# A row normalization on one core: a three-row first tile ahead of the 12-row tiles

## The chip, the cores and the metric

The kernel runs on one core of a Trainium2 chip. Times are microseconds of device time of one execution; the profile and its trace come from one profiled execution.

## What is computed

Every row of 1024 numbers is divided by the sum of its absolute values. There are 32 x 512 = 16,384 rows of float32, 67.1 MB in and 67.1 MB out.

```
x = randn(32, 512, 1024)                      # float32
sums = sum(abs(x), axis=-1, keepdims=True)
out = x / (sums + 1e-8)
```

## The kernel before

The 16,384 rows are spread over 128 partitions, so each partition has 128 rows to do. A tile takes R = 12 rows of each partition (128 x 12 x 4 KB, 6.3 MB): ten tiles of 12 rows and a last one of eight (`rows`). `piece(flat, i)` cuts tile i out of the flat tensor in such a way that the k rows of a partition lie side by side in memory, so that each partition's part of a transfer is one run of k x 4 KB.

The pool `sbuf` has four buffers of 12 rows (4 x 48 KB per partition), the pool `stats` small ones for the row sums. For each tile, in the order of the loop at the end of the function:

- SP issues the load into the next buffer (L72). Loads are alone on SP's queue. The fifth and later ones wait until the store of the tile four places earlier has landed, since that frees their buffer.
- VectorE reduces the tile to row sums of absolute values (L45), adds the small constant (L52), takes the reciprocal (L54), and multiplies the first half of the rows in place by it (L55; six of twelve rows).
- ScalarE multiplies the other rows in place, one instruction for each row (L62), and then issues the store of the tile (L74). Loads and stores so are on two queues, q1 from SP and q10 from ScalarE.

The order on each engine is the program's own (`tc.manual_schedule()`); nothing is reordered. DMA semaphores are taken from a set of eight and used again. The profile's numbers for a transfer count packets: each partition's run is one, 48 KB for a 12-row tile, and each of the 16 DMA engines carries eight of them for each transfer and ends it with a packet of four bytes for the semaphore.

Of the kernel before, what the change touches and what calls it, by code (L numbers as in the profile page):

```python
# [1 line left out]

# [4 lines left out]

FP32 = mybir.dt.float32
EPS = 1e-8


@with_exitstack
def kernel(
    ctx: ExitStack,
    tc: tile.TileContext,
    x: bass.AP,
    out: bass.AP,
):
    nc = tc.nc
    P = nc.NUM_PARTITIONS  # L20

    x_flat = x.flatten_outer_dims()
    out_flat = out.flatten_outer_dims()
    n, d = x_flat.shape


    R = 12
    BUFS = 4
    per_partition = n // P
    assert n % P == 0  # L30
    rows = [R] * (per_partition // R)
    if per_partition % R:
        rows.append(per_partition % R)

    def piece(flat, i):
        a, k = P * sum(rows[:i]), rows[i]
        return flat[a : a + P * k, :].rearrange("(p r) d -> p r d", p=P)

    sbuf = ctx.enter_context(tc.tile_pool(name="sbuf", bufs=BUFS))
    stats = ctx.enter_context(tc.tile_pool(name="stats", bufs=4))  # L40

    def normalize(x_tile, r0, k, kv):

        s = stats.tile([P, R], FP32)
        nc.vector.tensor_reduce(  # L45
            out=s[:, :k],
            in_=x_tile[:, r0 : r0 + k, :],
            axis=mybir.AxisListType.X,
            op=mybir.AluOpType.add,
            apply_absolute_value=True,  # L50
        )
        nc.vector.tensor_scalar_add(out=s[:, :k], in0=s[:, :k], scalar1=EPS)  # L52
        inv = stats.tile([P, R], FP32)
        nc.vector.reciprocal(out=inv[:, :k], in_=s[:, :k])  # L54
        nc.vector.tensor_mul(  # L55
            out=x_tile[:, r0 : r0 + kv, :],
            in0=x_tile[:, r0 : r0 + kv, :],
            in1=inv[:, :kv].unsqueeze(2).to_broadcast([P, kv, d]),
        )
        for r in range(kv, k):  # L60
            row = x_tile[:, r0 + r, :]
            nc.scalar.activation(  # L62
                out=row,
                in_=row,
                func=mybir.ActivationFunctionType.Copy,
                scale=inv[:, r : r + 1],
            )

    with tc.manual_schedule():
        for i, k in enumerate(rows):  # L70
            x_tile = sbuf.tile([P, R, d], FP32)
            nc.sync.dma_start(out=x_tile[:, :k, :], in_=piece(x_flat, i))  # L72
            normalize(x_tile, 0, k, k // 2)
            nc.scalar.dma_start(out=piece(out_flat, i), in_=x_tile[:, :k, :])  # L74


# [1 line left out]
_INS = ['x']  # L78
_OUTS = [((32, 512, 1024), 'float32')]


# [23 lines left out]
```

## Time and profile before

| what | before |
|---|---|
| median of 4 runs | 317.63 us (317.23 to 317.84) |
| the profiled execution | 317.3 us, its span 315.7 us |
| VectorE busy | 212.4 us, 67% of the span |
| ScalarE busy | 69.0 us, 22% |
| read from and written to HBM | 67.11 MB each, 425 GB/s over the span |
| the first load, issue to landing | 17.9 us |
| first store issued at | 38.78 us after the span's start |
| last store issued at | 295.13 us |
| load of 12 rows (6144 KB), issue to landing, median | 38.6 us |
| store of the same size, issue to landing, median | 53.3 us |

The span is the part of an execution between the first and the last instruction that the profiler saw; the execution's own time is 1.6 us longer. A landing time contains the waiting behind earlier transfers of the same queue, so it is much longer than the transfer. In the view of stretches, "GB/s" is what the DMA engines moved in that stretch, reading and writing together: a byte that is loaded or stored counts once, and the DMA share is the mean busy share of the 16 DMA engines. Packets are counted whole, so a stretch of a few microseconds can show a share a little above one.

### The profile page before, as it was taken

To read this page: it belongs to the slowest core of one execution; us is meant where nothing else is said; L and a number is where in the kernel's file an instruction comes from. 1 tells how busy PE (TensorE), PEld (TensorE's weight loads), DVE (VectorE), ACT (ScalarE), POOL (GpSimd) and SP (SyncE) were. 2 spreads that over 40 slices of the span, in tenths; PEclk is the share of its full clock that TensorE was granted. 3 is DMA by queue.
4 is the path that set the end of the run, shared out by engine and by line. 5 is a ranking of instruction groups with operands and counts; after the bars stand their busy time and mean duration, and the time that the engine had idled before them with its cause. 6 is when DMAs were issued, how large, how long until landed. Compare 5 with 4: busy or idle time off the path is not lost.

```text
span 315.7 us, 227 instructions
## 1 busy us (share of the span) xinstructions
DVE 212.4 (67%) x44; ACT 69.0 (22%) x65; POOL 0.2 (0%) x4
## 2 busy tenths in 40 slices
DVE  0069999999499079719944991797099449949300
ACT  0010804308007000700340070007003400611300
POOL 0000000000000000000000000000000000000000
DMA  8999999999999999999999999999999999999996
GB/s 305 480 405 430 461 380 424 405 473 417 405 480 411 411 473 411 424 455 424 436 436 424 437 448 411 430 442 424 436 448 411 436 428 448 436 440 436 417 430 282
DMA packets 3169, 134.23 MB, mean 425 GB/s; under 512 B 352, under 2 KB 352, under 8 KB 352
## 3 DMA queue, kind: packets, MB, share of 16 engines
q1 hardware_dynamic: 1584, 67.11, 49.8%
q10 hardware_dynamic: 1584, 67.11, 49.1%
q14 instruction: 1, 0.01, 0.0%
HBM read 67.11 MB, written 67.11 MB: 425 GB/s over the span
## 4 chain that ended last, share of the span: by engine, by line
DMA 55%; DVE 25%; another core or an unknown queue 9%; ACT 4%; issue 0%; SPq 0%; DVEq 0%; ACTq 0%
DMA x_tile<-in_x_dram 41%; DVE s L45 19%; DMA out_dram<-x_tile 14%; DVE x_tile L55 6%; ACT x_tile L62 4%; DVE inv L54 0%; DVE s L52 0%; SPq L72 0%; DVEq L54 0%; ACTq L74 0%
## 5 line engine op out<-in xcount | busy, mean ns | idle before, releaser
L45 DVE TENSOR_REDUCE s<-x_tile 128x12 f32<-128x12288 f32 (+1 forms) x11 | 138.2, 12564 | 81.0 <-DMA x_tile<-in_x_dram 81.0
L62 ACT ACTIVATE x_tile<-x_tile,inv 128x1024 f32<-128x1024 f32 x64 | 67.7, 1135 | 207.2 <-DVE inv L54 207.2
L55 DVE TENSOR_TENSOR x_tile<-x_tile,inv 128x6144 f32<-128x6144 f32 (+1 forms) x11 | 70.0, 6364 | 0.4
L62 ACT ACT_TABLE_LOAD x1 | 1.3, 1283 | 18.7 <-DMA x_tile<-in_x_dram 18.7
L54 DVE RECIPROCAL inv<-s 128x12 f32<-128x12 f32 (+1 forms) x11 | 2.5, 226 | 0.9
L52 DVE TENSOR_SCALAR s<-s 128x12 f32<-128x12 f32 (+1 forms) x11 | 1.9, 173 | 0.4
L89 POOL MEMSET const-bfloat16-1.0<- 128x1 bf16 x1 | 0.1, 101 | 0.0
L89 POOL MEMSET const-uint8-127<- 128x1 uint8 x1 | 0.1, 101 | 0.0
L89 POOL MEMSET const-float32-0.0<- 128x1 f32 x1 | 0.1, 98 | 0.2 <-issue 0.2
L89 POOL MEMSET const-float32-1.0<- 128x1 f32 x1 | 0.1, 98 | 0.0
## 6 DMA issues: line engine op xcount, KB each, us to landing
x_tile<-in_x_dram SPq DMA_DIRECT2D x10, 6144.0 KB, 38.6
out_dram<-x_tile ACTq DMA_DIRECT2D x10, 6144.0 KB, 53.3
x_tile<-in_x_dram SPq DMA_DIRECT2D x1, 4096.0 KB, 33.3
out_dram<-x_tile ACTq DMA_DIRECT2D x1, 4096.0 KB, 19.5
```

What stands on the lines that cost most here:

```text
L45: nc.vector.tensor_reduce(out=s[:, :k], in_=x_tile[:, r0 : r0 + k, :], axis=mybir.AxisListType.X, op=mybir.AluOpType.add, apply_absolute_v ...
L52: nc.vector.tensor_scalar_add(out=s[:, :k], in0=s[:, :k], scalar1=EPS)
L54: nc.vector.reciprocal(out=inv[:, :k], in_=s[:, :k])
L55: nc.vector.tensor_mul(out=x_tile[:, r0 : r0 + kv, :], in0=x_tile[:, r0 : r0 + kv, :], in1=inv[:, :kv].unsqueeze(2).to_broadcast([P, kv, d]),)
L62: nc.scalar.activation(out=row, in_=row, func=mybir.ActivationFunctionType.Copy, scale=inv[:, r : r + 1],)
L89: nc = _bacc.Bacc("TRN2", target_bir_lowering=False, num_devices=1)
```

## The change

The row list begins with a tile of three rows; the rest, 125 rows, is cut into ten tiles of 12 and a last one of five. The three-row tile has a buffer of its own in a new pool, so that the four 12-row buffers are free for the next four tiles. There are twelve tiles instead of eleven. Half of the rows, rounded down, go to VectorE as before: one of three in the first tile, two of five in the last.

```diff
     R = 12
     BUFS = 4
-    per_partition = n // P
+
+    FIRST = 3
     assert n % P == 0
-    rows = [R] * (per_partition // R)
-    if per_partition % R:
-        rows.append(per_partition % R)
+    full, last = divmod(n // P - FIRST, R)
+    rows = [FIRST] + [R] * full + ([last] if last else [])
...
     sbuf = ctx.enter_context(tc.tile_pool(name="sbuf", bufs=BUFS))
+    first = ctx.enter_context(tc.tile_pool(name="first", bufs=1))
     stats = ctx.enter_context(tc.tile_pool(name="stats", bufs=4))
...
         for i, k in enumerate(rows):
-            x_tile = sbuf.tile([P, R, d], FP32)
+            if i == 0:
+                x_tile = first.tile([P, FIRST, d], FP32)
+            else:
+                x_tile = sbuf.tile([P, R, d], FP32)
             nc.sync.dma_start(out=x_tile[:, :k, :], in_=piece(x_flat, i))
             normalize(x_tile, 0, k, k // 2)
             nc.scalar.dma_start(out=piece(out_flat, i), in_=x_tile[:, :k, :])
```

## The prediction

> **What bounds the kernel now.** I read the page's head and parts 2 and 3 first, since they say which resource is never free.
>
> ```profile
> span 315.7 us, 227 instructions
> DVE 212.4 (67%) x44; ACT 69.0 (22%) x65; POOL 0.2 (0%) x4
> ...
> DMA  8999999999999999999999999999999999999996
> ...
> q1 hardware_dynamic: 1584, 67.11, 49.8%
> q10 hardware_dynamic: 1584, 67.11, 49.1%
> ```
>
> VectorE is idle a third of the span and ScalarE three quarters, while the DMA row is full from the first slice to the last but one. The loads (q1) and the stores (q10) fill 49.8% + 49.1% = 98.9% of the time of 16 DMA engines: 312.2 of 315.7 us. The other 3.5 us are mostly the head before the first byte and the end after the last. Both queues moved the same bytes in the same packets, but the loads took 0.7% of 315.7 = 2.2 us longer per engine: this is the only waste inside the stream.
>
> Next come the stretches, to see whether a phase with loads alone is slower than one with both directions. The last two columns are the DMA share and GB/s.
>
> ```profile
> core 0: us, DVE busy (x) ACT busy (x) POOL busy (x), PEclk, DMA share, GB/s
> 0.00:1.70 1.70, 0.00 (x0) 0.00 (x0) 0.20 (x4) 1.00 0.00 0
> 1.70:16.20 14.50, 0.00 (x0) 0.00 (x0) 0.00 (x0) 1.00 1.05 431
> 16.20:40.00 23.80, 21.22 (x5) 7.62 (x7) 0.00 (x0) 1.00 0.99 430
> 40.00:45.00 5.00, 5.00 (x1) 0.00 (x0) 0.00 (x0) 1.00 0.96 324
> ...
> 112.20:141.20 29.00, 19.91 (x5) 6.34 (x6) 0.00 (x0) 1.00 1.01 434
> ...
> 281.40:303.40 22.00, 13.47 (x4) 4.26 (x4) 0.00 (x0) 1.00 0.99 429
> 303.40:314.30 10.90, 0.00 (x0) 0.00 (x0) 0.00 (x0) 1.00 0.89 385
> 314.30:315.70 1.40, 0.00 (x0) 0.00 (x0) 0.00 (x0) 1.00 0.00 0
> ```
>
> This is the deciding view. Loads alone (1.7 to 40 us) run at 430, loads with stores at 434, stores alone at 429. All 134.22 MB at 434 GB/s take 309.3 us, so the span is 1.7 (head) + 309.3 + 1.4 (end) and 3.3 us of loss. The packet records of the trace place the loss. A packet of 49,152 B normally takes 1.815 us. The eight packets per engine of the first load average 1.91 (a cold start, 0.76 us per engine); those of the third load, where the first store begins, average 1.95 (1.08 us: the stretch 40:45 with 324 GB/s). About 0.4 us is spread over later packets. The rest is that the 16 engines end between 313.1 and 314.3 us.
>
> Third, the waits of the load queue and the end of the timeline show how much cover the stream has.
>
> ```profile
> engine line waited for: us in total, times, longest us
> SPq L72 <- DMA out_dram<-x_tile: 226.5, 7, 54.6
> ```
>
> ```profile
> 281.39 8.69 DVE L45 TENSOR_REDUCE s<-x_tile 128x8 f32<-128x8192 f32 x1 [4.09 <-DMA x_tile<-in_x_dram]
> ...
> 290.62 4.42 DVE L55 TENSOR_TENSOR x_tile<-x_tile,inv 128x4096 f32<-128x4096 f32 x1
> 290.62 4.26 ACT L62 ACTIVATE x_tile<-x_tile,inv 128x1024 f32<-128x1024 f32 x4 [13.54 <-DVE inv L54]
> 295.13 0.34 ACTq L74 DMA_DIRECT2D out_dram<-x_tile  x1
> ```
>
> Loads do wait for stores to free a buffer, 226.5 us in all, but each is issued before its predecessor has drained: the fifth at 73.33 us, while the fourth's packets run to 81.0. The last store is issued at 295.13, and its first packet runs at 303.4, when the store before it is through. Nothing that VectorE, ScalarE or a buffer does lets the 16 engines run dry.
>
> **What the Trainium skill says.** Three places of the page "DMA: Bandwidth & Descriptors". "Issuing engines are not separate DMA queues": transfers issued from different engines run on the same 16 DMA engines. The trace agrees: the two queues' shares add up to 98.9%, and the store-only and load-only phases are as fast as the mixed one. "Where 436 GB/s comes from": the ports to SBUF give 435.2 GB/s in all; measured here 434. "Queues, rings and completion order": each engine alternates between queues packet by packet, whatever a packet's size. The trace agrees: the last load (8 rows, 32,768 B packets of 1.213 us) beside stores of 49,152 B needed 8 x (1.213 + 1.815) = 24.2 us, and the reduces that waited for the last two loads start 281.39 - 257.21 = 24.2 us apart.
>
> **The change, part by part.**
>
> *Bytes and phases.* Bytes stay. Storing begins near 13 us instead of 38.8, so the load-only phase shrinks; since it already runs at 430 of 434, with the rest of the gap in the cold start, this gains 0.
>
> *More packets.* Eleven tiles become twelve: per engine 8 more load packets and 8 more store packets. From 1.815 us for 49,152 B and 1.213 for 32,768 a packet's fixed part is 1.213 - 2 x (1.815 - 1.213) = 0.009 us, and successive packets begin 0.003 to 0.004 after the last. 16 x 0.0125 = 0.20 us. Each transfer ends with a 4-byte packet of 0.009 us per engine: 2 x 0.013 = 0.03. Sum +0.23 us, all on the path. No packet of 12,288 or 20,480 B is in the trace; the bounds are 0 and 1.0 us (32 such packets per engine each losing another 0.03); I take 0.23.
>
> *First tile.* Row cost from the groups of 12 and 8 rows: reduce (12.953 - 8.685)/4 = 1.067 per row and 0.15 fixed, so 3.35 us for three rows; scaling 1.067 per row on VectorE (one row, 1.2), 1.057 on ScalarE (two rows, 2.1). The load's packets are 0.46 us: 1.7 + 8 x 0.46 + 0.76 and the lag of the slowest engine give a landing near 6.7. Reduce, 0.45 for the two small steps, two ScalarE rows: the store is issued near 12.8. The 1.28 us table load hides under the reduce. These four VectorE instructions add some 0.5 us of fixed time to an engine with 100 us to spare: 0 on the path.
>
> *Five loads ahead instead of four.* SP now issues five loads without waiting for a buffer, 0.4 to 0.8 us each; were the fifth held up, SP has only loads behind it and 39 rows queued (47 us): 0. The waits added for reused semaphores name transfers long landed (the first load, the first store).
>
> *First store.* It alternates 12 KB packets with 48 KB load packets: 8 x (0.46 + 1.815) = 18 us, from about 17 to 35. The second tile lands near 21, VectorE needs 19.9, so the second store comes near 41.5. From 35 to 42 the store queue is empty; the loads cover this at full rate. The stall of a starting store queue, 1.08 us, moves from 40 to about 15 us and stays. Bounds for all starting stalls: C and B below.
>
> *Cover afterwards.* From 43 us a pair of tiles takes 29.0 us as before. The sixth load waits for the second store (landing 72.5) and is needed at 95; stores are issued 10 us or more ahead. At the end the 5-row load shares turns with 48 KB stores: 8 x (0.76 + 1.815) = 20.6 us, from 269.5 to 290. The tile before it, landed at 269.5, is stored from 289.5, needed at about 293.5: 4 us of cover, the thinnest place. The 5-row tile: 290.4 + 5.5 + 0.45 + 3.2 = 299.6, needed at 308. Both hold. The last packets, 20 KB, leave the engines' spread as it was: 0, with 0.4 either way.
>
> *Sum.* The profiled execution took 317.3 us, 1.6 around its span of 315.7; with +0.23 it would take 317.5. It lies 0.3 under the median of 317.63; on the median the forecast is 317.85.
>
> **The rivals.** A, the forecast: one stall, moved. 317.85, own range 317.3 to 318.4.
>
> B, slower: the stall is the price of a store queue that goes from empty to filled, not of the first store. Before, the queue never ran empty once begun; now it does near 35 us, and starts again near 42. For it: the stall hit all engines within a few microseconds of the first store. Against: the trace has only one such start, so a one-time cost explains it equally. Price 1.08 us once more: 317.85 + 1.08 = 318.93. It decides if the second store comes after the first is drained, which the times above say by 6 us; a second tile landing 6 us earlier would remove it.
>
> C, faster: both starting stalls scale with packet size, as if a first packet must be held whole before it goes on. With 12 KB instead of 48 KB three quarters of 0.76 + 1.08 vanish, -1.38: 316.5. Against: the first packets of the first load took 1.8 to 3.3 us, each engine another amount, rather like a latency.
>
> D: the thin cover at the end fails, or the engines' spread shifts; a microsecond of either sign. That the change doesn't do what it says is excluded: the instruction order shows a 128x3 reduce and a 128x3072 store first, 128x5 last.
>
> **How the numbers follow.** A 0.54, B 0.27, C 0.12, D 0.07 (0.05 slower, 0.02 faster). 0.2% is 0.64 us, about what a measurement of this kernel can tell from no change: faster is below 317.0, slower above 318.27. C and a little of D give faster 0.14; A gives same 0.54; B and D give slower 0.32. The range takes in A, B with its spread and the upper part of C: 316.8 to 319.2.
>
> **What would show it.** Right: the middle stretches at 434 again; the loss of GB/s near 15 us instead of 40; one loss, not two; queue shares still near 98.9% of the span. B: a second dip at 42 to 47 us and some 1 us more in the load queue's share. C: shares of both queues nearly equal. Wrong altogether: a stretch of some microseconds with neither queue moving, above all at 290 to 300.

## The result and the profile after

| what | before | after |
|---|---|---|
| median of the runs | 317.52 us (317.07 to 319.70, 62 runs) | 319.21 us (316.57 to 321.34, 44 runs) |
| middle half of the runs | 317.35 to 317.80 us | 317.49 to 319.72 us |
| profiled execution, its span | 317.3, 315.7 us | 316.65, 314.9 us |

The change makes the kernel slower by about a third of a per cent: ratio 1.0034, 95% interval 1.0021 to 1.0046. Ratios here and below leave out runs more than 1.5% above the fastest of their kernel: one of these 44, and three of the six of nudge. This one is that of the means (318.75 and 317.68 us). The medians stand at 1.0053, because half of the runs after lie above 319 us with a tail of quick ones. What stands out is not the shift but the width: the runs after reach from 1 us under the median of before to 4 us over it. And the profiled execution is one of the quickest: its span is 0.8 us *shorter* than that of before. A profile of one execution cannot explain this result by itself; it shows what a good execution looks like, and a second profile, further down, shows a longer one.

The page of the changed kernel, the quick execution:

```profile
span 314.9 us, 237 instructions
## 1 busy us (share of the span) xinstructions
DVE 212.1 (67%) x48; ACT 70.1 (22%) x66; POOL 0.2 (0%) x4
...
DMA  7989999999999999999999999999999999999997
...
q1 hardware_dynamic: 1728, 67.11, 49.8%
q10 hardware_dynamic: 1728, 67.11, 49.3%
q14 instruction: 2, 0.02, 0.0%
```

The picture of before is unchanged: VectorE idle a third, the DMA row full, both queues together 99.1% of the span. 1728 packets instead of 1584 are the 128 + 16 of the twelfth transfer in each direction.

Stretches of the same execution (the last two columns are DMA share and GB/s):

```profile
core 0: us, DVE busy (x) ACT busy (x) POOL busy (x), PEclk, DMA share, GB/s
...
1.70:16.20 14.50, 4.92 (x4) 3.47 (x3) 0.00 (x0) 1.00 1.06 434
16.00:24.00 8.00, 0.35 (x1) 0.00 (x0) 0.00 (x0) 1.00 0.97 389
...
35.00:42.00 7.00, 6.90 (x4) 4.90 (x5) 0.00 (x0) 1.00 1.04 449
42.00:50.00 8.00, 8.00 (x2) 1.45 (x2) 0.00 (x0) 1.00 0.93 393
92.00:121.00 29.00, 19.91 (x4) 6.34 (x6) 0.00 (x0) 1.00 1.00 434
121.00:150.00 29.00, 19.91 (x4) 6.35 (x6) 0.00 (x0) 1.00 1.00 434
```

The loss that lay at 40 to 45 us is now at 16 to 24, where the three-row store begins; the middle runs at 434 GB/s as before. The 393 at 42 to 50 us looks like a second loss where the store queue fills again. It is at least partly the counting of whole packets: the stretch before it has 449. By the packet records the packets that begin at 44 to 52 us are lengthened by 0.18 us per engine in this execution and by 0.01 in the longer one below, against the 1.08 that rival B asks for.

The end of the timeline of the same execution:

```profile
267.17 12.96 DVE L46 TENSOR_REDUCE s<-x_tile 128x12 f32<-128x12288 f32 x1 [8.93 <-DMA x_tile<-in_x_dram]
...
287.35 0.34 ACTq L78 DMA_DIRECT2D out_dram<-x_tile  x1
287.74 5.49 DVE L46 TENSOR_REDUCE s<-x_tile 128x5 f32<-128x5120 f32 x1 [0.48 <-DMA x_tile<-in_x_dram]
...
297.01 0.34 ACTq L78 DMA_DIRECT2D out_dram<-x_tile  x1
```

The last 12-row store is issued at 287.35; by the packet records its first packet runs at 292.2. The thin place has 4.8 us of cover, and it holds.

### The profile page after: what moved, and what is told of

It is laid out like the page before. It is cut to its first block, busy times and chain, and to the rows that moved or that the text cites. A ratio compares the mean times of both kernels' runs of the same rounds, so it can differ in the third digit from the quotient of the medians.

```text
span 314.9 us, 237 instructions
## 1 busy us (share of the span) xinstructions
DVE 212.1 (67%) x48; ACT 70.1 (22%) x66; POOL 0.2 (0%) x4
## 3 DMA queue, kind: packets, MB, share of 16 engines
q1 hardware_dynamic: 1728, 67.11, 49.8%
q10 hardware_dynamic: 1728, 67.11, 49.3%
## 4 chain that ended last, share of the span: by engine, by line
DMA 61%; DVE 23%; another core or an unknown queue 9%; ACT 1%; SPq 0%; issue 0%; DVEq 0%; ACTq 0%
DMA x_tile<-in_x_dram 47%; DVE s L46 18%; DMA out_dram<-x_tile 13%; DVE x_tile L56 4%; ACT x_tile L63 1%; SPq L76 0%; DVE inv L55 0%; DVE s L53 0%; DVEq L55 0%; ACTq L78 0%
## 5 line engine op out<-in xcount | busy, mean ns | idle before, releaser
L46 DVE TENSOR_REDUCE s<-x_tile 128x12 f32<-128x12288 f32 (+2 forms) x12 | 138.4, 11530 | 82.2 <-DMA x_tile<-in_x_dram 82.2
L63 ACT ACTIVATE x_tile<-x_tile,inv 128x1024 f32<-128x1024 f32 x65 | 68.9, 1136 | 219.8 <-DVE inv L55 219.8
L56 DVE TENSOR_TENSOR x_tile<-x_tile,inv 128x6144 f32<-128x6144 f32 (+2 forms) x12 | 69.1, 5758 | 0.7 <-DVE inv L55 0.3
L55 DVE RECIPROCAL inv<-s 128x12 f32<-128x12 f32 (+2 forms) x12 | 2.6, 220 | 1.0
L53 DVE TENSOR_SCALAR s<-s 128x12 f32<-128x12 f32 (+2 forms) x12 | 2.1, 173 | 0.4
```

Of the source, the lines that this page charges most:

```text
L46: nc.vector.tensor_reduce(out=s[:, :k], in_=x_tile[:, r0 : r0 + k, :], axis=mybir.AxisListType.X, op=mybir.AluOpType.add, apply_absolute_v ...
L56: nc.vector.tensor_mul(out=x_tile[:, r0 : r0 + kv, :], in0=x_tile[:, r0 : r0 + kv, :], in1=inv[:, :kv].unsqueeze(2).to_broadcast([P, kv, d]),)
L63: nc.scalar.activation(out=row, in_=row, func=mybir.ActivationFunctionType.Copy, scale=inv[:, r : r + 1],)
```

## The experiments

Theories at the start: *restart* (rival B, the store queue that runs empty pays the stall again), *thin cover* (part of rival D), and *small packets* (12 KB packets beside 48 KB ones). Later came *addresses* (every tile lies three rows further on in memory), *five loads ahead* (the extra buffer lets a fifth load queue early), *stagger* (the order in which the start leaves the 16 engines decides whether one falls back later) and *lone engine* (an engine whose turns run against those of the others falls further back). Each ratio compares with runs of the kernel before that were made beside it. "Middle half" leaves out the lowest and the highest quarter of the runs.

| run | median us | lowest to highest, runs | middle half | ratio to before, 95% |
|---|---|---|---|---|
| again_a | 318.54 | 316.50 to 319.72, 14 | 317.56 to 319.34 | 1.0022 (1.0003 to 1.0041) |
| hold | 317.96 | 316.40 to 320.78, 14 | 317.10 to 318.69 | 1.0022 (0.9997 to 1.0046) |
| gap | 324.17 | 323.75 to 325.41, 4 | | 1.0215 (1.0200 to 1.0231) |
| moved | 318.65 | 316.64 to 320.66, 22 | 317.55 to 319.52 | 1.0027 (1.0007 to 1.0047) |
| nobuf | 319.35 | 316.69 to 320.76, 22 | 318.19 to 319.68 | 1.0044 (1.0027 to 1.0061) |
| splitload | 317.74 | 317.51 to 318.49, 14 | 317.68 to 317.89 | 1.0000 (0.9986 to 1.0013) |
| splitstore | 318.33 | 317.05 to 320.64, 14 | 317.57 to 318.93 | 1.0013 (0.9992 to 1.0034) |
| late | 318.39 | 317.00 to 320.15, 14 | 318.21 to 318.53 | 1.0021 (1.0006 to 1.0036) |
| eightfirst | 324.79 | 322.33 to 325.89, 6 | | 1.0216 (1.0183 to 1.0249) |
| firstsix | 323.24 | 320.06 to 324.53, 6 | | 1.0140 (1.0095 to 1.0185) |
| nudge | 326.76 | 321.60 to 327.58, 6 | | 1.0198 (1.0136 to 1.0260) |

**again_a and again_b: the changed kernel again.** No edit.

> The changed kernel once more, since its times spread from 316.6 to 321.3 us and the profile at hand is of one of the quickest executions. Theory restart (rival B): a profile of a longer execution shows GB/s lost at 43 to 50 us, where the store queue fills again, and nothing lost elsewhere. Theory thin cover (rival D): the loss lies at 285 to 300 us. Theory small packets: it lies at 15 to 36 us, while the 12 KB packets of the first store run beside 48 KB loads. Median near 319 us in all three.

> The changed kernel a third time, for a further profile of an execution; same expectations as for the first repetition.

The profile of again_a is again of a quick execution (316.50 us). again_b is a longer one: 319.19 us, next to the median of the 44 runs. Its page:

```profile
span 317.4 us, 237 instructions
...
q1 hardware_dynamic: 1728, 67.11, 49.4%
q10 hardware_dynamic: 1728, 67.11, 48.9%
```

98.3% of 317.4 is 312.0 us of packet time per engine; the quick execution had 99.1% of 314.9, which is 312.1 (the packet records, without the rounding, give 312.0 and 311.8). On the mean of the 16 engines the longer execution *moves its bytes in the same engine time* to within 0.2 us. So its 2.5 us are not a stream that is slower on all engines: they are time in which most engines have nothing left to do. Where:

```profile
core 0: us, DVE busy (x) ACT busy (x) POOL busy (x), PEclk, DMA share, GB/s
...
16.00:24.00 8.00, 0.00 (x0) 0.00 (x0) 0.00 (x0) 1.00 0.92 361
...
42.00:50.00 8.00, 8.00 (x2) 1.92 (x2) 0.00 (x0) 1.00 1.01 436
92.00:121.00 29.00, 19.91 (x4) 6.34 (x6) 0.00 (x0) 1.00 1.00 434
...
285.00:300.00 15.00, 13.10 (x5) 7.97 (x8) 0.00 (x0) 1.00 1.01 435
```

No dip at 42 to 50 us, against restart; no dip at 285 to 300, against thin cover. The 361 at 16 to 24 fits small packets, but the packet records put only 0.92 us per engine of lengthening between 8 and 60 us, as in the quick execution (0.94). What differs is the last 3.6 us; again_b, then the quick execution of the changed kernel, then the kernel before:

```profile
312.70:313.80 1.10, 0.00 (x0) 0.00 (x0) 0.00 (x0) 1.00 0.40 168
313.80:316.30 2.50, 0.00 (x0) 0.00 (x0) 0.00 (x0) 1.00 0.08 33
```

```profile
312.70:313.80 1.10, 0.00 (x0) 0.00 (x0) 0.00 (x0) 1.00 0.09 37
313.80:316.30 2.50, 0.00 (x0) 0.00 (x0) 0.00 (x0) 1.00 0.00 0
```

```profile
312.70:313.80 1.10, 0.00 (x0) 0.00 (x0) 0.00 (x0) 1.00 0.28 119
313.80:316.30 2.50, 0.00 (x0) 0.00 (x0) 0.00 (x0) 1.00 0.00 0
```

In again_b data still move for 2.5 us at a share of 0.08: 1.3 engines of 16. The packet records name no engine, but a packet begins within 9 ns of its predecessor's end, so they can be strung into 16 chains. These are the times at which each of the 16 engines sends its last packet (us), and the packet time after 60 us beyond the usual 1.815 us per 48 KB that the most affected engines collect. The times are those of the 16 semaphore packets of the last store and need no stringing; where engines change packets together the chains can be swapped, so the smaller figures on the right are rough:

```
                 last packets of the 16 engines                  largest excess after 60 us
before           313.1 ... (14 engines) ... 314.2 314.3          0.5  0.5  0.6  0.7
after, quick     312.8 ... (14 engines) ... 313.5 313.6          0.0  0.1  0.2  0.4
again_b          312.7 ... (13 engines) ... 313.8 315.2 316.3    0.2  0.3  1.6  2.6
hold             312.8 ... (13 engines) ... 313.7 314.9 315.5    0.3  0.5  1.3  1.9
moved            312.7 ... (13 engines) ... 314.5 314.9 316.9    0.5  0.9  1.2  3.2
late             313.1 ... (14 engines) ... 314.1 315.4          0.2  0.3  0.8  1.3
splitload        313.0 ... (14 engines) ... 314.6 315.1          0.2  0.2  0.9  1.4
```

The time of an execution is that of its slowest engine: in the profiles of before, of the changed kernel and of hold, moved, nobuf, late, splitload and splitstore the mean of the 16 times lies at 313.2 to 313.8 us, the latest of them at 313.5 to 316.9. In again_b 14 engines are done by 313.8; one is 2.5 us later. Most of its excess comes in packets that follow a change from one transfer to the next: +0.24 us at 104.0, +0.47 at 162.2, +0.40 at 191.7, +0.72 at 221.1, each on the load packet right behind the semaphore packet of a store. From 60 to 90 us this engine runs against the majority of the other 15, loading while they store and the reverse, in 0.64 of the time, and is the only one over a half. In the two quick profiles three and five engines were out of step with the rest (0.70 to 0.76 of the time), and nobody lost more than 0.4 us; the kernel before is split into seven and nine, and the excess is 0.0 to 0.7 us on each. This suggests an engine that is alone out of step, but splitload, a kernel without a small store, speaks against it: its two late engines run against the others in only 0.34 and 0.31 of the time from 60 to 90 us, and in 0.64 and 0.79 from 210 to 265, when they are behind. There the step is lost as the lateness grows, rather than before it. Why an engine is held up the trace does not tell.

**hold: same tiles, the store queue starts once.**

```diff
             normalize(x_tile, 0, k, k // 2)
+            if i == 0:
+                held = x_tile
+                continue
+            if i == 1:
+                nc.scalar.dma_start(out=piece(out_flat, 0), in_=held[:, :FIRST, :])
             nc.scalar.dma_start(out=piece(out_flat, i), in_=x_tile[:, :k, :])
```

> The changed kernel with its same tiles, but the store of the three-row tile is held back and issued just before that of the second tile, so the store queue starts once and never runs empty. Theory restart: the spread goes, median 317 to 317.6 us. Theory small packets: the 12 KB store still runs beside 48 KB loads, from 44 us on, and the spread stays, median near 319. Theory thin cover: the end is as before the hold, spread and 319 stay.

The spread stays (316.40 to 320.78), and the profile has two late engines, of which one is out of step early (0.55 of the time from 60 to 90 us) and the other is not (0.28). Restart falls: without any empty stretch of the store queue the runs are as wide. The median is lower than the changed kernel's, but with 14 runs of such width this is not settled.

**gap: the kernel before with an empty stretch of the store queue.** The first tile's store is cut by partitions, 16 at once and 112 with the second store.

```diff
+            if i == 0:
+                nc.scalar.dma_start(out=piece(out_flat, 0)[:16], in_=x_tile[:16, :k, :])
+                held = x_tile
+                continue
+            if i == 1:
+                nc.scalar.dma_start(out=piece(out_flat, 0)[16:], in_=held[16:, :R, :])
```

> The kernel before with its eleven tiles; the store of its first tile is split: 16 partitions at 38.8 us (one 48 KB packet for each DMA engine), the other 112 partitions just before the second tile's store at 58.7 us. The store queue runs empty for some 14 us and starts again, with no small packet anywhere. Theory restart: 318.5 to 319.2 us and a spread like that of the changed kernel. Theories small packets and thin cover: 317.5 to 317.8 us, as the kernel before.

324.17 us, far beyond either expectation. The cut changed more than the timing: while the 112-partition store ran, single store packets took up to 6.7 us instead of 1.8. This run decides nothing about restart; a store cut by partitions is not the same store in two parts.

**moved: the old addresses for the 12-row tiles.**

```diff
-        a, k = P * sum(rows[:i]), rows[i]
+        k = rows[i]
+        r0 = R * full if i == 0 else R * full + FIRST if k == last else R * (i - 1)
+        a = P * r0
```

> The changed kernel with the same tiles in the same order, but the ten 12-row tiles take the first 120 rows of each partition's share (as in the kernel before, each tile at a multiple of 6 MB), and the three-row and five-row tiles take the last eight. Theory addresses (an engine that falls back does so because the shift of all tiles by three rows makes loads and stores meet in HBM): the spread goes, 316.5 to 317.5 us. Theory stagger (the engines' order, left by the quick start with small packets, decides whether one of them falls back during the even middle part): spread and median stay, near 318.5 to 319.

As wide as the changed kernel. The shift by three rows in memory is not the cause.

**nobuf: without the buffer of its own.**

```diff
-            if i == 0:
-                x_tile = first.tile([P, FIRST, d], FP32)
-            else:
-                x_tile = sbuf.tile([P, R, d], FP32)
+            x_tile = sbuf.tile([P, R, d], FP32)
```

> The changed kernel without the extra buffer: the three-row tile takes one of the four buffers, so four loads instead of five run ahead and the fifth waits for the small store. Theory five loads ahead (loads that are queued early leave load and store changes in another phase): median back to 317.5 us or less with a small spread. Theories addresses and stagger: as the changed kernel, 318.5 to 319.

319.35 us and as wide. The fifth load ahead is not the cause, and the extra buffer brings nothing that these runs can tell.

**splitload: only the small first load, in the kernel before.**

```diff
-            nc.sync.dma_start(out=x_tile[:, :k, :], in_=piece(x_flat, i))
+            if i == 0:
+                nc.sync.dma_start(out=x_tile[:, :3, :], in_=piece(x_flat, i)[:, :3, :])
+                nc.sync.dma_start(out=x_tile[:, 3:k, :], in_=piece(x_flat, i)[:, 3:, :])
+            else:
+                nc.sync.dma_start(out=x_tile[:, :k, :], in_=piece(x_flat, i))
```

> The kernel before; only the load of its first tile is issued as two, three rows and nine rows, so that the stream begins with the same 12 KB packets as in the changed kernel. All tiles, addresses, buffers and stores are those of before. Theory stagger from the small first load: the engines end the first load close together, the stalls at the start shrink a little, and the spread of the changed kernel appears (up to 320). Theories addresses, five loads ahead, early store: 317.2 to 317.8 us, as before.

317.51 to 318.49 us in 14 runs, beside 316.90 to 320.06 us in 51 runs of the kernel before. A small load at the start does not widen the runs. The profile is of the slowest of them (318.49 us) and has two late engines, at 314.6 and 315.1 us: late engines occur without a small store too, and the kernel before has its own slow runs, up to 319.70, of which no profile was taken.

**splitstore: only a small first store, in the kernel before.**

```diff
+            if i == 0:
+                nc.scalar.dma_start(out=piece(out_flat, 0)[:, :3, :], in_=x_tile[:, :3, :])
+                nc.scalar.dma_start(out=piece(out_flat, 0)[:, 3:, :], in_=x_tile[:, 3:, :])
+                continue
```

> The kernel before; only the store of its first tile is issued as two, three rows and nine rows, back to back at 38.8 us. Theory small store (the 12 KB store packets beside 48 KB load packets shift the engines' turns against each other): the spread of the changed kernel appears, median 318.2 to 319.2. If it stays at 317.3 to 317.8 us with a small spread, neither the small load alone nor the small store alone brings the spread, and it needs the tile sequence as a whole.

The middle half widens to 1.4 us, where 19 runs of the kernel before beside it have 0.4; the extremes do not differ (317.05 to 320.64 against 317.06 to 320.26). The mean shift is not resolved (the interval includes 1). Tile sizes, addresses, buffers and the end are those of before. On its own 14 runs this is weak evidence that a short store among long loads widens the runs; it fits the other kernels with enough runs: the five with such a store (the changed one, hold, moved, nobuf, splitstore) have middle halves of 1.4 to 2.2 us, the three without (before, splitload, late) 0.2 to 0.7. The profile, of a quick execution (317.32 us), has no late engine: the last ends at 314.3.

**late: the changed kernel without a small store among loads.**

```diff
+            if i == 0:
+                held = x_tile
+                continue
+            if i == len(rows) - 1:
+                nc.scalar.dma_start(out=piece(out_flat, 0), in_=held[:, :FIRST, :])
```

> The changed kernel with all its tiles, buffers and its small first load, but the store of the three-row tile is held to the end and issued just before the last store, when loads are over. So no 12 KB store packets take turns with 48 KB load packets, and storing begins with a 12-row store near 41 us. Theory small store (the short store packets put single engines out of step): the spread goes and the gain of the quickest executions stays, 316.3 to 317.3 us, below both kernels. Theory tile sequence (small load, tiles shifted, five-row end): the spread stays, median 318 to 319.5 us. Theory restart is settled the same way as in the other held kernel: the store queue starts once.

Half right. The middle half shrinks to 0.3 us (318.21 to 318.53), with one run under and one over. But it sits at 318.4, not at 316.3 to 317.3; the theory of the tile sequence had the median at 318 to 319.5. The kernel is still slower than before, by 0.06 to 0.36%; the changed kernel was so by 0.03 to 0.41% in again_a. So the small store among loads goes with the width, but taking it away does not bring the time back. In its profile the stall of the starting stores is the dearest of all (1.49 us per engine between 8 and 60 us; 0.94 in the quick execution, 1.07 before), and one engine ends 1.3 us behind the others, though from 60 to 90 us none runs against the majority in more than 0.39 of the time. As storing starts later here, late changes the start as well. Why its time should repeat from run to run is open.

**eightfirst and firstsix: other first tiles.** Rows 8, then ten times 12; and 6, ten times 12, 2, both with four buffers.

```diff
-    rows = [R] * (per_partition // R)
-    if per_partition % R:
-        rows.append(per_partition % R)
+    rows = [8] + [R] * (per_partition // R)
```

> The kernel before with the eight-row tile first instead of last: no packet under 32 KB, no extra buffer, every 12-row tile shifted by eight rows (4 MB), storing begins near 27 us and the store queue does not run empty. Theory addresses: a spread like that of the changed kernel. Theories small packets, stagger from a small first load, five loads ahead: 317.2 to 318 us.

> Rows 6, ten times 12, 2, with the four buffers of before and no extra one: store packets of 24 KB, store queue not empty in between. If the spread needs packets as small as 12 KB or an empty store queue: 316.5 to 317.5 us, below both kernels. If any short first tile brings it: 318 to 319.5 us. The last 12-row tile's store keeps 3 to 5 us of cover; if that is gone, a stretch with neither queue moving shows near 293 us.

Both miss, for another reason that their stretches show; eightfirst first, then firstsix:

```profile
285.00:302.60 17.60, 15.71 (x4) 2.35 (x3) 0.00 (x0) 1.00 0.82 355
302.60:307.70 5.10, 4.21 (x1) 3.99 (x4) 0.00 (x0) 1.00 0.00 0
307.70:322.50 14.80, 0.00 (x0) 0.00 (x0) 0.00 (x0) 1.00 0.99 425
```

```profile
290.00:299.50 9.50, 9.33 (x4) 4.80 (x5) 0.00 (x0) 1.00 0.64 278
299.50:302.00 2.50, 2.50 (x2) 1.54 (x2) 0.00 (x0) 1.00 0.00 0
302.00:320.30 18.30, 3.01 (x4) 1.15 (x1) 0.00 (x0) 1.00 0.94 402
```

Here thin cover is real: a share of 0.00 for 5.1 and 2.5 us, with VectorE and ScalarE at work on the last 12-row tile and no transfer left. eightfirst ends on a 12-row tile, whose 20 us of compute nothing covers. In firstsix the last 12-row store is issued at 301.34, when the store queue has been empty since 299.6; three engines also fell back by 3 us. Both say little on the small store, and much on the end: the five-row tail of the changed kernel was safe by 4.8 us.

**nudge: hold one engine up in the kernel before.**

```diff
+    spare = ctx.enter_context(tc.tile_pool(name="spare", bufs=1))
...
+            if i == 3:
+                extra = spare.tile([P, 384], FP32)
+                nc.sync.dma_start(out=extra[:17, :], in_=x_flat[:17, :384])
```

> The kernel before with one extra, useless load behind the fourth: 17 partitions x 1.5 KB into a spare tile, a shape meant to fall on one DMA engine alone and to hold that engine up by about 1.2 us near 81 us. Nothing reads it. Theory lone engine (an engine that is out of step with the others is stretched again at every change of transfer and falls further back): the nudged engine loses 1 to 3 us more by the end; median 318.5 to 320 us with a spread like that of the changed kernel. Theory plain delay: the 1.2 us stay 1.2, partly inside the engines' spread of 1.1 us: 317.6 to 318.7 us, small spread.

```profile
280.00:305.00 25.00, 19.56 (x5) 10.15 (x10) 0.00 (x0) 1.00 0.94 407
305.00:316.00 11.00, 0.03 (x1) 0.00 (x0) 0.00 (x0) 1.00 0.90 387
316.00:325.60 9.60, 0.00 (x0) 0.00 (x0) 0.00 (x0) 1.00 0.08 34
```

26 KB of useless data cost 4 to 10 us (9 by the medians; the profile is of a 327.24 us run), and they are spent as the stretches show: 14 engines are done by 316.4 and for 9.6 us the share is 0.08. The packets did fall on one engine (q1 counts 1602 packets: 1584, the 17 and a single semaphore packet), but my price was wrong. Each of the 17 took its turn against a whole 48 KB store packet, so the loads behind them waited from 83 to 115 us, and the store packets between were longer than usual. By 125 us this engine was 7 us behind, not 1.2. Then a second engine, which had no extra packet, lost 7.7 us, most of it between 169 and 203. So this is no clean test of lone engine; it shows how far single engines can fall behind a stream that is otherwise full, and what that costs.

## Why the prediction was right or wrong

By the ratio the time lies inside the range, on its slower side: 1.0034 x 317.52 is 318.6 us, and the range was 316.8 to 319.2. The median of the runs, 319.21, lies on its very edge. The likeliest case (no measurable difference) was wrong, and the slower side came by the mechanism that had got the least chance. That the range holds it is luck in part, since its upper end was set for rival B.

- *What bounds it, and that an earlier store gains nothing*: right. 434 GB/s in the middle, 99.1% and 98.3% of the span in the two queues.
- *More packets, +0.23 us*: consistent. The new packets take 0.46 and 0.76 us as worked out; nothing in the runs resolves 0.2 us. The sum itself misreads one thing: in the records a packet begins 0.003 us before its predecessor ends, not after, so the term comes to about 0.11 us.
- *First tile*: landing at 7.0 us (6.7 forecast), store issued at 13.02 (12.8), its packets from 17.0 to 34.4 (17 to 35). The second tile landed at 23.6, not 21: the turns given to the small store and the stall both fall on its load. So the second store came at 43.75, not 41.5, and the store queue carried nothing for longer than I said (34.4 to 47.4 us). It cost nothing that the runs show.
- *The stall moves and stays*: right in kind; 0.94 us per engine against 1.07. With the cold start (0.65 against 0.77), the later excess (0.03 against 0.35) and engines that end closer together, this makes the quick executions 0.8 us quicker. A small gain that I had at 0.
- *Cover at the end, 4 us*: right (4.8), and the load of five rows took 20.6 us as forecast (287.74 - 267.17, the two reduces that waited). The two kernels with other tails show that this term decides as soon as it turns negative.
- *Rival B, restart*: its number (318.93) is near the outcome, its mechanism is refuted by hold and by the packet records, which lose only 0.01 to 0.18 us where the store queue starts again. A near number would have hidden this.
- *Rival C*: not what happened; the stalls shrank by a tenth or two, not by three quarters.
- **The step that failed**: "The last packets, 20 KB, leave the engines' spread as it was: 0, with 0.4 either way", and rival D, which named the spread, at 0.07. The engines' ends lie up to 3.6 us apart (again_b), and by how much differs from execution to execution. I treated the 16 engines as one pipe of 434 GB/s. They are 16 pipes with fixed shares of the work: what one loses, no other takes over. In again_b the latest engine carries 96 load and 96 store packets like the others, and ends 2.5 us after fourteen of them.

What is shown: the longer executions that were profiled owe their time to one to three late engines; a small store among the loads goes with wide runs, in the kernel before and in the changed one, and the runs are narrow where it is taken out; restart, addresses and the fifth load are not the cause of the width. What is only argued: that short packets of one queue among long ones of the other put single engines out of step, and that an engine alone out of step is held up at each change of transfer; splitload and late count against the second. Open: the mechanism of the hold-up, and what makes the changed kernel slower on the mean, since late is slower too, without the small store among the loads; a five-row end without a small first tile was not tried. The picture of the late engines rests on a handful of profiles.

## What to carry to other kernels

The stream here kept all DMA engines full and gained nothing by starting one direction earlier; ask first whether the one-way phase is slower than the mixed one. When the total is fixed, look at the slowest engine: if the queues' busy time is unchanged and the span is longer, either the stream has a hole, as in eightfirst, or the engines no longer end together, as in again_b; the stretches tell which. And compare a single profile with the spread of the runs before believing it: here it showed an execution 0.8 us quicker of a kernel that is slower.

## What the runs showed of the hardware that was not expected

- Two queues took turns packet by packet with packets of 1.5 and 48 KB: seventeen of 1.5 KB held the loads behind them on one engine for 32 us (nudge).
- A transfer of 17 partitions ran on one DMA engine alone; all 17 packets stand in one chain, with a single semaphore packet (nudge).
- The second instruction fetch of 8 KB falls inside the span of the changed kernel, at 297.8 us (the q14 line of the page: 2, before 1). It takes 0.31 us on one engine and lengthens that engine's next packet by 0.36; near the end it counts if it meets the slowest engine.
- The same program's executions spread over 4.8 us (44 runs) where a sibling with the same bytes (splitload) spreads over 1.0 (14 runs) and the kernel before over 2.6 (62 runs).
